# A decoder layer on one core: x loaded transposed with its rows between the chunks, and the retention's key and value projections beside the lower half of the sparse attention

## The chip, the cores and the metric

The kernel runs on one core of a Trainium2 chip. Its engines are TensorE (PE; weight loads PEld), VectorE (DVE), ScalarE (ACT), GpSimd (POOL) and SyncE (SP, which here only issues DMA transfers); each takes its own instructions in order and waits on semaphores for the others. The metric is device time in microseconds (us) of one execution.

## The reference, cut to what matters

One layer on x of 1024 rows by 1024 columns in fp32: an RMS norm, one wide input projection, three groups of heads, a SiLU gate, an output projection, a residual add and a last norm.

```python
u = rms_norm(h, attn_norm[layer])
proj = jnp.einsum('bsd,dc->bsc', u, w_in[layer])
(dq, dk, dv, sq, ckv, iq, ik, iw, rq, rk, rv, gate) = jnp.split(proj, split_points, axis=-1)
...
o_a = diff_attention(dq, dk, dv, ...)          # 6 heads, two softmaxes each
o_b = dsa_attention(sq, rms_norm(ckv), iq, ik, iw, w_uk, w_uv, top_k)   # 8 index heads pick 256 keys per query
o_c = retention(rotary(rq), rotary(rk), rv, ret_norm[layer])            # 4 heads, chunks of 128
y = jax.nn.silu(gate) * mixed
h = h + jnp.einsum('bsc,cd->bsd', y, w_out[layer])
```

RMS norm divides each row of x by the root of its mean square and multiplies each column by a gain.

## The kernel before

u is kept transposed (columns of x on the partitions, rows along the free axis) as two fp32r tiles, `uh` (the rounded value) and `ul` (the rest), each [128, 8 chunks, 1024 rows]. Weights are split in the same way, and every projection multiplies three times: high by high, high by low, low by high. `split` does it: a copy to the high part, a subtraction for the low.

**Front.** `setup` loads x in eight blocks of 128 rows (tiles `x`, on SP's queue) and, after the first two, the weights of the differential attention's values and of the index keys and head weights (`wide`, 456 columns). `prep_a` squares and sums a block on ACT, works out 1/rms in `rstd_small` (tiny operations on ACT and DVE), and multiplies the block by 1/rms and by the gain (`gb`, broadcast to all partitions) on DVE. `prep_b` transposes it on PE in eight 128x128 pieces (L220) and splits the result from PSUM into `uh` (ACT) and `ul` (DVE). Then `gemm` runs the 456 columns, row block by row block: 8 x 8 x 3 = 192 matmuls of 128x456 (L282 to L284). `dv_evac` takes each block from PSUM: the values `v`, the index keys `kt`, which are transposed into `kkh` and `kkl`, and the head weights `iw`.

**Index stage.** `iq0` to `iq3` are projections of the index queries; `idx_scores` makes the scores from them and `kkh`, `kkl`.

**Middle stage.** Three streams are interleaved: the differential attention (`diff`, L651), the top-k search with its ties, and the remaining projections in the order of K's strings `order` and `order2` (g: gates, q and k: differential queries and keys, s: sparse queries, ck: the latent, M: what is made of it, r: the retention's query, key and value). `rv` and `rk` are the last two of them: 192 matmuls of 128x256 each (L282 to L284 again).

**Lower half of the sparse attention.** `dsa(p, 0)` for three pairs of heads takes the four lower row blocks: 24 steps, each of score matmuls (L720, L721), a softmax on DVE (L728, L736) and ACT (L729), transposes on PE (L611) and value matmuls (L626). Beside it run the ties of the other blocks and a third stream: `retention(0)`, then `out_weights`, which loads w_out in sixteen pieces through two buffers (`wr`) and splits them into `woh` and `wol`, and part of the output projection of block 7 (`project`, L935 to L937). `woh` and `wol` take the memory of `uh` and `ul`, so their first write waits for the last matmul that reads u.

**Upper half.** `dsa(p, 1)`, 24 steps on the four larger blocks, beside `retention(1)` and two projected blocks; then the rest of the projection.

What sets the order: the code emits the streams by `interleave`, which takes next from the stream that has used the smallest share of its planned cost (`wd`, `wt`, `wg`, `gw` ... in K), and a scheduler at build time places the instructions on each engine by a model of their readiness; inside `manual_schedule` the named engines keep the order of the code.

Of the kernel before, what the change touches and what calls it, by code (L numbers as in the profile page):

```python
# [10 lines left out]
F = mybir.dt.float32  # L11
# [7 lines left out]
S = 1024  # L19
# [12 lines left out]
K = {'mk': 'up ky', 'mp': 's2 g5 g4', 'rt': ('hl', 'pq'), 's0': ('gg', 'gg', 'ag', 'gg', 'vg', 'gg', 'vg', 'vg'), 'xp': 2, 'bufs': (8, 3, 3, 5, 3, 4, 1), 'pp': (7,), 'rot': 0, 'order': 'g0 g1 k1 q1 k2', 'order2': 'q2 g2 rq g6 s0 ck g7 s1 M g3 rv rk | ', 'wd': 36, 'wt': 13, 'wg': 119, 'gw': 56, 'rw': 26, 'rx': 132, 'pw': 40, 'ow': 84, 'nf': 2, 'ev': 200, 'late': 8, 'de': ('aa', 'aa', 'aa'), 'da': 'ax', 'gd': (7, 4, 2), 'hlp': 'sqkk', 'tkp': '', 'vt': 'v', 'rs': 'x', 'nv': 1, 'dn': 'v', 'ws': 'gg', 'oe': ('av', 'gg'), 'one': 0, 'idx': (42, 40), 'iqs': 'iq2 iq3 q0 k0'}  # L32
# [36 lines left out]
class Trunk:  # L69
# [65 lines left out]
    def setup(self):  # L135
# [4 lines left out]
        self.gb = self.ptile(1024)  # L140
        nc.scalar.dma_start(self.gb, bass.AP(tensor=i["attn_norm"].tensor, offset=i["attn_norm"].offset,
                                             ap=[[0, 128], [1, 1024]]))
        self.x = {}
        for b in range(NB):
            self.x[b] = self.slot("x", [128, 1024])
            nc.sync.dma_start(self.x[b], i["x"][0, b * 128:(b + 1) * 128, :])
            if b == K["xp"] - 1:
                self.wide()
# [13 lines left out]
    def setup_late(self):  # L162
# [25 lines left out]
        m1 = self.sb.tile([128, NB, 72], F, name="trigdec", tag="m1")  # L188
# [4 lines left out]
    def rstd_small(self, ss, n, tag):  # L193
# [7 lines left out]
        nc.vector.scalar_tensor_tensor(q, r, v, r, op0=OP.mult, op1=OP.mult)  # L201
# [4 lines left out]
    def prep_a(self, b):  # L206
        nc = self.nc
        xt = self.x[b]
        junk = self.half("junk", [128, 1024], BF)
        ss = self.sb.tile([128, 1], F, name=self.name("ss"), tag="ss", bufs=2)  # L210
        nc.scalar.activation(junk, xt, AF.Square, accum_out=ss)
        r = self.rstd_small(ss, D, "rs1")
        nc.vector.scalar_tensor_tensor(xt, xt, r, self.gb, op0=OP.mult, op1=OP.mult)

    def prep_b(self, b):
        nc = self.nc
        xt = self.x.pop(b)
        p = self.pS()
        for k in range(KC):
            nc.tensor.transpose(p[:, k * 128:(k + 1) * 128], xt[:, k * 128:(k + 1) * 128], self.ident)  # L220
# [759 lines left out]
```

## Time and profile before

| | |
|---|---|
| runs | 785.86, 781.14, 777.98 us; median 781.14 us |
| profiled execution | 785.29 us, of which the span on the page is 783.6 us |
| PE, PEld | 724.2 us (92%), 597.4 us (76%) |
| DVE, ACT, POOL | 551.5 us (70%), 447.6 us (57%), 311.5 us (40%) |
| moved by DMA | 113.05 MB, 144 GB/s over the span |
| matmuls of the 512-wide projections (L130 to L132) | 3 x 352, 141.6, 139.4 and 140.7 us busy |

The page shows busy time by engine; matmuls are pipelined, so two that overlap are both counted to their ends, and a full PE can still be slow. A view by stages shows in which stretch an engine had room, at what granted clock PE ran and what the transfers moved. A row of the timeline gives the start, the length, the line, the operation with its tiles (out<-in), and in brackets how long the engine had stood and who released it. In the views by line, the numbers are a count, then busy time and mean, or the least, median and greatest length in ns.

### The profile page before, as it was taken

How to read it: one execution, taken by the hardware profiler on the slowest of the kernel's cores; microseconds unless marked ns; L12 is line 12 of the kernel's file. 1: busy time of each engine (PE TensorE's matmuls, PEld its weight loads, DVE VectorE, ACT ScalarE, POOL GpSimd, SP SyncE). 2: the span in 40 equal slices, each digit the busy share in tenths (PEclk: the TensorE clock that was granted, in tenths of full speed). 3: DMA queues.
4: the chain of work that ended last, by engine and by line, in shares of the span. 5: the costliest groups of instructions: out<-in, count | busy, mean ns of one | idle time of the engine just before them, and what ended most of it. 6: DMA issues, size and time to landing. Idle time of an engine off the chain costs nothing.

```text
span 783.6 us, 12891 instructions
## 1 busy us (share of the span) xinstructions
PE 724.2 (92%) x4314; PEld 597.4 (76%) x4314; DVE 551.5 (70%) x1312; ACT 447.6 (57%) x989; POOL 311.5 (40%) x343
## 2 busy tenths in 40 slices
PE   3999999999999999988799789998978999999996
PEld 3798888887887898766577567997855887787884
DVE  5920277789999989999889997325657766664443
ACT  4531255559888968787755566434356656554332
POOL 6401322225434438557347699335733242120000
PEclk9999999999999999999899999999968999999999
DMA  9303645454374352461274476564578974413351
GB/s 332 78 1 71 197 136 145 139 137 132 99 218 115 85 163 78 120 169 35 67 206 144 144 215 190 158 192 160 158 213 236 281 200 127 123 48 108 118 176 59
DMA packets 93250, 113.05 MB, mean 144 GB/s; under 512 B 11904, under 2 KB 63488, under 8 KB 93056
## 3 DMA queue, kind: packets, MB, share of 16 engines
q1 hardware_dynamic: 91888, 109.61, 48.1%
q10 hardware_dynamic: 1296, 2.62, 0.9%
q8 instruction: 34, 0.56, 0.3%
q14 instruction: 32, 0.26, 0.1%
HBM read 75.50 MB, written 36.18 MB: 143 GB/s over the span
## 4 chain that ended last, share of the span: by engine, by line
PE 61%; DVE 16%; DMA 6%; issue 6%; POOL 5%; ACT 4%; SPq 0%; DVEq 0%; POOLq 0%; ACTq 0%
PE pB L626 6%; PE pG L130 6%; PE pG L132 6%; PE pG L131 5%; PE pB L611 4%; PE pG L282 4%; PE pG L936 4%; PE pG L937 4%; PE pG L935 4%; PE pG L283 4%; PE pG L284 4%; DVE jv L378 3%; DMA wr<-in_w_in_dram 2%; PE pS L344 2%; PE pS L343 2%
## 5 line engine op out<-in xcount | busy, mean ns | idle before, releaser
L130 PE MATMUL pG<-uh,wh 128*128 128x512 f32 x352 | 141.6, 402 | 1.8 <-DVE gt L827 1.8
L132 PE MATMUL pG<-uh,wl 128*128 128x512 f32 x352 | 140.7, 400 | 0.6 <-POOL wl L123 0.6
L131 PE MATMUL pG<-ul,wh 128*128 128x512 f32 x352 | 139.4, 396 | 0.0
L123 POOL TENSOR_TENSOR wl<-wr,wh 128x512 fp32r<-128x512 f32 x56 | 79.3, 1430 | 106.3 <-PE pG L131 69.4
L392 ACT ACTIVATE ja<-sc,tk_c 128x896 int8<-128x896 f32 (+2 forms) x93 | 83.2, 895 | 17.3 <-DVE tk_c L399 12.0
L113 ACT ACTIVATE pt<-pB 128x512 f32<-128x512 f32 (+2 forms) x120 | 58.8, 496 | 43.8 <-PE pB L611 43.5
L130 PEld LDWEIGHTS pG<-uh,wh 128*128 128x128 f32 x352 | 66.8, 190 | 16.4 <-DVE gt L827 2.4
L132 PEld LDWEIGHTS pG<-uh,wl 128*128 128x128 f32 x352 | 66.4, 189 | 16.1 <-POOL wl L123 0.9
L611 PE MATMUL pB<-ident,pp 128*128 128x128 f32 x432 | 72.9, 287 | 5.5 <-DVE gt L758 3.4
L626 PE MATMUL pB<-pt,v 128*64 128x128 f32 x864 | 70.8, 302 | 7.6 <-ACT pt L113 7.0
L131 PEld LDWEIGHTS pG<-ul,wh 128*128 128x128 f32 x352 | 66.7, 189 | 13.0 <-issue 0.2
L626 PEld LDWEIGHTS pB<-pt,v 128*64 128x64 f32 x864 | 57.7, 147 | 18.9 <-ACT pt L113 9.5
L378 DVE TENSOR_SCALAR_CACHE_REDUCE jv<-sc,tk_c 128x640 bf16<-128x640 f32 (+4 forms) x81 | 69.2, 855 | 1.0
L611 PEld LDWEIGHTS pB<-ident,pp 128*128 128x128 f32 x432 | 51.2, 144 | 22.2 <-issue 9.1
L677 POOL TENSOR_SCALAR pq<-pq,mx 128x896 f32<-128x896 f32 (+7 forms) x48 | 43.2, 901 | 58.6 <-DVE mx L676 55.8
L119 POOL TENSOR_SCALAR wh<-wr 128x512 fp32r<-128x512 f32 x56 | 37.8, 680 | 59.9 <-DMA wr<-in_w_in_dram 54.3
L282 PE MATMUL pG<-wh,uh 128*128 128x256 f32 x192 | 55.0, 288 | 2.6 <-POOL wh L119 2.6
L283 PE MATMUL pG<-wl,uh 128*128 128x256 f32 x192 | 54.9, 286 | 0.0
L284 PE MATMUL pG<-wh,ul 128*128 128x256 f32 x192 | 54.3, 284 | 0.0
L346 ACT ACTIVATE pp<-pS 128x1024 f32<-128x1024 f32 (+5 forms) x48 | 36.5, 760 | 31.1 <-PE pS L344 31.0
L651 PE MATMUL pS<-st,st 128*128 128x512 f32 (+3 forms) x144 | 43.3, 368 | 11.5 <-DVE mx L662 8.9
L351 DVE SCALAR_TENSOR_TENSOR sc<-pp,iw,sc 128x1024 f32<-128x1024 f32 (+5 forms) x42 | 43.5, 1044 | 14.3 <-ACT pp L346 13.6
(218 smaller groups left out, 1756.1 us busy)
## 6 DMA issues: line engine op xcount, KB each, us to landing
wr<-in_w_in_dram SPq DMA_DIRECT2D x56, 256.0 KB, 3.2
st<-qdq SPq DMA_DIRECT2D x24, 256.0 KB, 4.2
st<-qkk SPq DMA_DIRECT2D x18, 256.0 KB, 5.9
x<-in_x_dram SPq DMA_DIRECT2D x8, 512.0 KB, 6.6
qiq<-hl SPq DMA_DIRECT2D x16, 256.0 KB, 3.5
st<-qiq SPq DMA_DIRECT2D x8, 512.0 KB, 3.3
wr<-in_w_out_dram SPq DMA_DIRECT2D x16, 256.0 KB, 3.4
xr<-in_x_dram SPq DMA_DIRECT2D x8, 512.0 KB, 3.5
```

The source lines that it names most:

```text
L113: self.nc.scalar.activation(out, in_, AF.Copy)
L123: (self.nc.vector if e2 == "v" else self.nc.gpsimd).tensor_tensor(lo, src, hi.bitcast(F), OP.subtract)
L130: mm(ps, wh, xh, start=start, stop=False)
L131: mm(ps, wh, xl, start=False, stop=False)
L132: mm(ps, wl, xh, start=False, stop=stop)
L282: mm(ps, uh, hs[k], start=k == 0, stop=False)
L283: mm(ps, uh, ls[k], start=False, stop=False)
L284: mm(ps, ul, hs[k], start=False, stop=k == KC - 1)
L378: nc.vector.tensor_scalar(jv[:, :nv[b]], hb if b == 7 and bit >= 16 else sc[b], t, 0.0, op0=op, op1=OP.add, accum_out=cnt[:, j:j + 1])
L392: nc.scalar.activation(ja[:, :nv[b]], sc[b], AF.Sign, bias=cut(b), scale=-1.0, accum_out=cnt[:, cols[b]:cols[b] + 1])
L611: nc.tensor.transpose(p[:, k], pr[:, (k0 + k) * 128:(k0 + k + 1) * 128], self.ident)
L626: self.last = nc.tensor.matmul(o[u * 64:(u + 1) * 64], vals[k], pts[g, a][:, k, u * 128:(u + 1) * 128], start=k == (i if u else 0), stop=k ...
```

## The change

The host now also passes x transposed (`x_t`), the 456 weight columns as one array (`w_dv`) and the gain as a column per chunk (`gk`). `setup` loads the eight chunks of `x_t` (tiles `x`, the first two in halves) on SP's queue with the eight blocks of rows of x between them, and the weights on ACT's queue; `square` sums the squares of each row block on ACT. `front` multiplies before the norm is known: `split_x` makes `uh` and `ul` from x times gain, and for each chunk as it comes PE runs 18 matmuls for six row blocks, which take six PSUM banks. Row blocks 6 and 7 follow in a second pass over the chunks. 1/rms of the rows (`rn`) multiplies these results as they leave PSUM (`evac`). For all other projections u must hold the norm: `row_rms` spreads 1/rms over the partitions with eight matmuls of ones by diagonal tiles (`diags`), and `resplit` multiplies x by gain and 1/rms and splits it again, first rows 0 to 511, then 512 to 1023. The order on PE, DVE and SP in `front` is that of the code. `keys` (the transposes of the index keys) stands between iq0 and iq1.

In K, `order2` was `'q2 g2 rq g6 s0 ck g7 s1 M g3 rv rk | '` and is `'q2 g2 rq g6 s0 ck g7 s1 M g3 | rv rk'`: what stands behind the bar is run ahead of `retention(0)` in the third stream of the lower half. That stream's planned cost `gw` goes from 56 to 97. `s0`, which names the engines that split each chunk of the 456 columns, uses POOL and ACT and no longer DVE.

```diff
+        self.gk = self.const("gk", [128, KC])
+        nc.scalar.dma_start(self.gk, i["attn_norm"])
+        self.wide()
+        self.x, self.rows = [], []
+        self.ss = self.const("ss", [128, NB])
+        for k in range(KC + 1):
+            if k < KC:
+                t = self.slot("x", [128, S])
+                for c in (slice(0, 512), slice(512, S)) if k < 2 else (slice(0, S),):
+                    nc.sync.dma_start(t[:, c], i["x_t"][k * 128:(k + 1) * 128, c])
+                self.x.append(t)
+            for b in ((k - 1,) if 0 < k else ()):
+                row = self.ptile(D) if b % 2 else self.wtile("row", [D], F)
+                nc.sync.dma_start(row, i["x"][0, b * 128:(b + 1) * 128, :])
+                self.rows.append(row)
+                self.square(b)
...
+    def split_x(self, k):
+        g = self.gk[:, k:k + 1]
+        for c in (slice(0, 512), slice(512, S)):
+            hi, x = self.uh[:, k, c], self.x[k][:, c]
+            nc.scalar.activation(hi, x, AF.Copy, scale=g)
+            nc.vector.scalar_tensor_tensor(self.ul[:, k, c], x, g, hi.bitcast(F), op0=OP.mult, op1=OP.subtract)
...
+    def row_rms(self):
+        p = self.pS()
+        for b in range(NB):
+            nc.tensor.matmul(p[:, b * 128:(b + 1) * 128], self.ct, self.dg[b], start=True, stop=True)
...
+            self.nc.vector.tensor_scalar(self.dg[b], self.ident, self.rn[:, b:b + 1], None, op0=OP.mult)
...
+    def resplit(self, p, half):
+        c = slice(half * 512, half * 512 + 512)
+        for k in range(KC + 1):
+            if k < KC:
+                x = self.x[k][:, c]
+                nc.vector.scalar_tensor_tensor(x, x, self.gk[:, k:k + 1], p[:, c], op0=OP.mult, op1=OP.mult)
+                nc.scalar.activation(self.uh[:, k, c], x, AF.Copy)
+            if k:
+                hi = self.uh[:, k - 1, c]
+                nc.vector.tensor_tensor(self.ul[:, k - 1, c], self.x[k - 1][:, c], hi.bitcast(F), OP.subtract)
...
+        for k in range(KC):
+            self.split_w(k)
+            self.split_x(k)
+            if k == KC - 1:
+                self.diags()
+            step(range(6), k)
+        for b in range(6):
+            evac(b, ps[b])
+        rb = self.row_rms()
+        self.resplit(rb, 0)
+        ps[6:] = [self.pG()[:, :WA] for _ in range(2)]
+        for k in range(KC):
+            step((6, 7), k)
+        for b in (6, 7):
+            evac(b, ps[b])
+        self.resplit(rb, 1)
+        return keys
...
+            r = self.rn[:, b:b + 1]
+            nc.scalar.activation(self.v[:, b, :], ps[:, 0:384], AF.Copy, scale=r)
+            nc.scalar.activation(kt[:, b], ps[:, 384:456], AF.Copy, scale=r)
...
-        for b in range(NB):
-            self.prep_a(b)
-            self.prep_b(b)
-        drain(self.gemm(("a", C_DV, WA, self.dv_evac())))
-        with self.tc.manual_schedule(engines={mybir.EngineType.PE}):
-            drain(units("iq0 iq1"))
+        with self.tc.manual_schedule(engines={et.PE, et.DVE, et.SP}):
+            keys = self.front()
+        with self.tc.manual_schedule(engines={et.PE}):
+            drain(units("iq0"))
+            keys()
+            drain(units("iq1"))
```

How the instructions move, at three places (`order` rows: line, operation, out<-in, shape, count). The first is PE from the start of the program: `pS` receives the transposes of row blocks `x`, `pG` the 456 columns of one row block. Before:

```order
L220 MATMUL pS_129<-ident,x_77 128x128 x8
L220 MATMUL pS_151<-ident,x_79 128x128 x8
L282 MATMUL pG_321<-wb_299,uh 128x456
L283 MATMUL pG_321<-wb_301,uh 128x456
L284 MATMUL pG_321<-wb_299,ul 128x456
```

And PE in the changed kernel where the last chunk ends: `pB_164` is row block 5, `pS_387` the spread 1/rms, `pG_420` and `pG_421` are row blocks 6 and 7.

```order
L272 MATMUL pB_164<-wb_153,uh 128x456
L272 MATMUL pB_164<-wb_157,uh 128x456
L272 MATMUL pB_164<-wb_153,ul 128x456
L233 MATMUL pS_387<-dg_347,ct 128x128 x4
L233 MATMUL pS_387<-dg_352,ct 128x128 x4
L272 MATMUL pG_420<-wb_152,uh 128x456
L272 MATMUL pG_421<-wb_152,uh 128x456
```

The transposes at the head are gone; the spread of 1/rms stands between the first six row blocks and the last two.

The second place is PE at the end of rk in the kernel before (`pG_5371` is rk's last row block, `pS` are score steps of the lower half):

```order
L282 MATMUL pG_5371<-wh_5128,uh 128x256
L283 MATMUL pG_5371<-wl_5129,uh 128x256
L284 MATMUL pG_5371<-wh_5128,ul 128x256
L626 MATMUL pB_5839<-pt_5812,v_5629 64x128 x3
L611 MATMUL pB_5863<-ident,pp_5821 128x128
L720 MATMUL pS_5903<-st_5890,st_5891 128x512
L721 MATMUL pS_5903<-st_5890,st_5891 128x512
L720 MATMUL pS_5922<-st_5890,st_5891 128x128
L721 MATMUL pS_5922<-st_5890,st_5891 128x128
```

And PE inside rk's last row block (`pG_6137`) in the changed kernel, whose L347 to L349, L787, L788, L693 and L678 are the same operations:

```order
L347 MATMUL pG_6137<-wh_5893,uh 128x256
L348 MATMUL pG_6137<-wl_5894,uh 128x256
L787 MATMUL pS_5657<-st_5651,st_5652 128x384
L693 MATMUL pB_5526<-pt_5493,v_5066 64x128 x3
L678 MATMUL pB_5562<-ident,pp_5500 128x128 x3
L788 MATMUL pS_5657<-st_5651,st_5652 128x384
L349 MATMUL pG_6137<-wh_5893,ul 128x256
L347 MATMUL pG_6137<-wh_5903,uh 128x256
```

Nine of the lower half's 24 score steps stood ahead of rk's last matmul; now 17 do, spread through rv and rk.

The third place is ACT at the first copy into `woh`. Before (`pp` and `mx` are a step's softmax, `pt` its transposed result):

```order
L113 ACTIVATE pt_5812<-pB_5827 128x4x128
L729 ACTIVATE pp_5900,mx_5899<-pp_5900,mx_5899 128x384
L113 ACTIVATE woh<-wr_5722 128x512
L113 ACTIVATE pt_5862<-pB_5863 128x128
L113 ACTIVATE pt_5862<-pB_5868 128x2x128
```

In the changed kernel (L796 is the same softmax):

```order
L113 ACTIVATE pt_5561<-pB_5562 128x3x128
L796 ACTIVATE pp_5588,mx_5587<-pp_5588,mx_5587 128x256
L113 ACTIVATE woh<-wr_6183 128x512
L113 ACTIVATE pt_5561<-pB_5579 128x4x128
L796 ACTIVATE pp_5661,mx_5660<-pp_5661,mx_5660 128x384
```

The copy stood ahead of the softmax of the lower half's tenth step, and stands ahead of that of the seventeenth now.

## Rows read from the trace of the kernel before

**Rows 1.** Stages of the whole span: length, each engine's busy us, PEclk, DMA share, GB/s.

```profile
0.00:10.00 10.00, 0.08 (x1) 0.11 (x2) 2.67 (x16) 4.00 (x8) 2.44 (x9) 1.00 0.79 274
10.00:20.00 10.00, 7.76 (x30) 6.87 (x31) 8.54 (x10) 4.92 (x9) 10.00 (x11) 1.00 1.05 392
...
30.00:40.00 10.00, 8.77 (x41) 7.63 (x42) 9.19 (x26) 4.05 (x12) 0.75 (x1) 0.83 0.01 3
...
176.00:494.00 318.00, 293.79 (x1694) 238.51 (x1693) 291.69 (x739) 235.97 (x535) 182.43 (x190) 0.97 0.49 136
...
494.00:525.00 31.00, 31.00 (x268) 29.46 (x267) 8.76 (x32) 13.71 (x39) 9.10 (x10) 1.00 0.55 175
...
546.00:559.50 13.50, 13.50 (x113) 12.75 (x113) 6.72 (x14) 1.38 (x4) 11.49 (x18) 1.00 0.37 116
559.50:602.50 43.00, 34.72 (x211) 24.30 (x210) 27.63 (x91) 23.83 (x64) 14.27 (x16) 0.80 0.75 215
```

**Rows 2.** PE's timeline in the front: start us, us, line, operation, count.

```profile
9.92 1.94 PE L220 MATMUL pS<-ident,x 128*128 128x128 f32 x8 [9.92 <-DVE rs L198]
...
28.24 1.04 PE L220 MATMUL pS<-ident,x 128*128 128x128 f32 x8
...
33.50 0.58 PE L282 MATMUL pG<-wb,uh 128*128 128x456 f32 x1
33.88 0.58 PE L283 MATMUL pG<-wb,uh 128*128 128x456 f32 x1
...
63.88 0.37 PE L282 MATMUL pG<-wb,uh 128*128 128x456 f32 x1
64.08 0.37 PE L283 MATMUL pG<-wb,uh 128*128 128x456 f32 x1
...
67.10 0.39 PE L130 MATMUL pG<-uh,wh 128*128 128x512 f32 x1
...
78.36 0.40 PE L130 MATMUL pG<-uh,wh 128*128 128x512 f32 x1
```

**Rows 3.** The chain of waits around rk's weights: start us, us, what.

```profile
525.67 5.51 DMA wr<-in_w_in_dram
```

**Rows 4.** Groups by line, first 70 us: count, busy us, mean ns, idle before.

```profile
L213 DVE SCALAR_TENSOR_TENSOR x<-x,rs,pp 128x1024 f32<-128x1024 f32 x8 | 13.0, 1628 | 0.2
...
L123 DVE TENSOR_TENSOR ul<-pS,uh 128x1024 fp32r<-128x1024 f32 x8 | 9.7, 1217 | 5.1 <-ACT uh L113 5.1
```

**Rows 5.** Timeline of ACT and DVE, the first row block: start us, us.

```profile
6.01 1.06 ACT L211 ACTIVATE junk<-x 128x1024 bf16<-128x1024 f32 x1 [3.93 <-DMA x<-in_x_dram]
...
8.49 1.28 DVE L213 SCALAR_TENSOR_TENSOR x<-x,rs,pp 128x1024 f32<-128x1024 f32 x1
```

**Rows 6.** Two lines and tile woh: count, ns min/median/max, first and last start.

```profile
L441 PE MATMUL pB<-f,bd x12: 590/592/697, 295.9 to 537.0; 128*128 128x512 f32 x12
...
L448 DVE SCALAR_TENSOR_TENSOR f<-f,c_diff_norm,f x6: 751/1414/1632, 303.0 to 546.0; 128x512 f32<-128x512 f32 x6
...
L123 DVE TENSOR_TENSOR wol<-wr,woh x8: 672/689/1540, 560.5 to 610.0; 128x512 fp32r<-128x512 f32 x8
...
L113 ACT ACTIVATE woh<-wr x8: 616/629/631, 559.4 to 609.3; 128x512 fp32r<-128x512 f32 x8
...
L119 POOL TENSOR_SCALAR woh<-wr x8: 617/648/805, 559.5 to 610.4; 128x512 fp32r<-128x512 f32 x8
...
L123 POOL TENSOR_TENSOR wol<-wr,woh x8: 1267/1279/1609, 560.2 to 611.2; 128x512 fp32r<-128x512 f32 x8
```

**Rows 7.** PE's timeline in rv, and thirty value matmuls near the end.

```profile
494.77 0.29 PE L282 MATMUL pG<-wh,uh 128*128 128x256 f32 x1
494.89 0.28 PE L283 MATMUL pG<-wl,uh 128*128 128x256 f32 x1
...
717.02 1.96 PE L626 MATMUL pB<-pt,v 128*64 128x128 f32 x30
```

**Rows 8.** ACT's timeline behind rk: start us, us, idle before, and releaser.

```profile
559.43 0.63 ACT L113 ACTIVATE woh<-wr 128x512 fp32r<-128x512 f32 x1 [9.90 <-PE pG L283]
```

More of the change, by code (lines that the diff above doesn't have):

```diff
@@ L216, in prep_b, with square @@
+    def square(self, b):
+        junk = self.half("junk", [128, D], BF)
+        self.nc.scalar.activation(junk, self.rows[b], AF.Square, accum_out=self.ss[:, b:b + 1])
+    def row_rms(self):
         nc = self.nc
-        xt = self.x.pop(b)
         p = self.pS()
-        for k in range(KC):
-            nc.tensor.transpose(p[:, k * 128:(k + 1) * 128], xt[:, k * 128:(k + 1) * 128], self.ident)
-        pv = p.rearrange("p (k s) -> p k s", k=KC)
-        sl = slice(b * 128, (b + 1) * 128)
-        self.split(self.uh[:, :, sl], self.ul[:, :, sl], pv)
+        for b in range(NB):
+            nc.tensor.matmul(p[:, b * 128:(b + 1) * 128], self.ct, self.dg[b], start=True, stop=True)
+        return p
@@ new lines, in diags @@
+    def diags(self):
+        self.rn = self.rstd_small(self.ss, D, "rs8")
+        self.dg = []
+        for b in range(NB):
+            if b % 4 == 0:
+                dgs = self.half("dg", [128, 4, 128])
+            self.dg.append(dgs[:, b % 4])
+            self.nc.vector.tensor_scalar(self.dg[b], self.ident, self.rn[:, b:b + 1], None, op0=OP.mult)
+    def resplit(self, p, half):
+        nc = self.nc
+        c = slice(half * 512, half * 512 + 512)
[7 more added lines that the diff above has]
+                nc.vector.tensor_tensor(self.ul[:, k - 1, c], self.x[k - 1][:, c], hi.bitcast(F), OP.subtract)
@@ new lines, in front, with step @@
+    def front(self):
+        nc = self.nc
+        hs, ls = self.wsplit(C_DV, WA)
+        evac, keys = self.dv_evac()
+        mm = nc.tensor.matmul
+        big = [self.pS(), self.pS()]
+        ps = [big[b // 2][:, b % 2 * 512:b % 2 * 512 + WA] for b in range(4)] + [self.pB()[:, :WA] for _ in range(2)]
+        ps += [None, None]
+        def step(blocks, k):
+            st, sp = k == 0, k == KC - 1
+            todo = [[(b, self.uh, hs, st, False) for b in blocks], [(b, self.uh, ls, False, False) for b in blocks],
+                    [(b, self.ul, hs, False, sp) for b in blocks]]
+            order = [t for b in zip(*todo) for t in b] if sp else [t for w in todo for t in w]
+            for b, u, w, s0, s1 in order:
+                mm(ps[b], u[:, k, b * 128:(b + 1) * 128], w[k], start=s0, stop=s1)
+        for k in range(KC):
+            self.split_w(k)
[14 more added lines that the diff above has]
+        return keys
@@ L231, in wide @@
     def wide(self):
-        raws = []
+        self.dvw = []
         for k0 in range(0, KC, 2):
@@ L249, in wsplit @@
             ls = [big[2 + k // 2][:, k % 2] for k in range(KC)]
-            for k in range(KC):
-                self.split(hs[k], ls[k], self.dvw[k // 2][:, k % 2], *K["s0"][k])
+            self.split_w = lambda k: self.split(hs[k], ls[k], self.dvw[k // 2][:, k % 2], *K["s0"][k])
             return hs, ls
```

63 lines of the change are left out of this document (26 added, 37 removed).

## The prediction

> **What bounds the kernel now.** I read the stages first [rows 1]. TensorE is busy for 724 of 783.6 us, so idle engines elsewhere matter little; what can be won is the time in which PE is idle, slow, or not yet started. The stages differ. The index scores up to 176 us stay the same work in the same order. From 176 to 494 us DVE has 292 of 318 us busy: that stage is set by DVE and the chains around it, and in the order its instructions stand as before, so I only shift it. Two places are left, and the change is at both. The first is the front, up to 67 us. PE starts at 9.92 us, does its first transposes with gaps, and falls to the lower clock after it has stood: at 33 us the 128x456 matmuls follow each other every 0.38 us, where the granted clock of 30 to 40 us averages 0.83 (a mix of 1.2 and 2.4 GHz), against 0.206 us later [rows 1, 2]. The second is 494 to 602.5 us: rv and rk run there with PE full, except for a wait of some 7 us for rk's weights (a load of 5.51 us, then a split) [rows 3], and what follows, 559.5 to 602.5 us, has PE at 34.7 of 43 us with a granted clock of 0.80 and only 211 matmuls, where 113 fit in the 13.5 us before [rows 1].
>
> **The front, before.** 192 matmuls of 128x456 at 0.206 us are 39.6 us; 64 transposes, eight in 1.04 us or, without the tail of the last, 0.87, are 7 us [rows 2]. From the first transpose to iq0's first matmul at 67.10 us there are 57.2 us, so some 11 us are gaps and slow clock. iq1 starts at 78.36 us [rows 2], and that is the point I compare.
>
> **The front, after.** The 64 transposes go, with their eight copies on ACT, eight subtractions (1.22 us) and eight normalizations (1.63 us) on DVE [rows 4]. x arrives twice: 4.19 MB transposed and 4.19 MB in rows; with 1.87 MB of value weights and 0.52 MB for iq0 that is 10.8 MB ahead of or with the last row block. The traffic of before, 274 GB/s in the first 10 us and 392 in the next [rows 1], gives 6.66 MB by 20 us and the rest by 30.6 us; the last transposed chunk, 9.2 MB in, lands at about 26.5 us. The first half-chunk is half of the 512 KB transfer that ACT had at 6.01 us [rows 5]; with a split behind it PE starts at about 6 us.
>
> PE: six blocks x eight chunks x three = 144 matmuls, 29.7 us, plus 1.6 us for some nine at 0.38 us at the start, before the clock rises: 37.2 us. A chunk feeds 18 matmuls, 3.7 us, and arrives about every 2.8 us (the 1.05 MB of a chunk and its row block at 392 GB/s), so PE, not the transfer, sets this once it runs. Per chunk ACT needs two copies of 0.63 us [rows 6] and a square of 1.06 us [rows 5], DVE two operations of about 0.65 us: both hidden below 3.7 us. The row statistics (30.6; the square and small operations, 2.5 us from 6.01 to 8.49 in the trace [rows 5]; then eight diagonal products of about 0.25 us) are ready at about 35 us, 2 us early; that is their cover. Ahead of them DVE waits for the tiny load of c_diff_norm, behind it for dl, both queued among these loads on SP; dl should land at about 36 us.
>
> Eight fp32 matmuls with ones broadcast 1/rms: the 128x512 one lasts 0.59 us [rows 6], so 0.9 us (a quarter each) to 4.7 us (full price); I take 2: 39.2 us. Now u is multiplied again, in two halves: 32 DVE operations of 128x512. Nearest rows: 0.61 us (half of 1.22 [rows 4]), 0.67 to 0.69 and 0.75 us [rows 6]; I take 0.65, so 10.4 us a half. PE covers the first half with blocks 6 and 7 (48 matmuls, 9.9 us, to 49.1). ACT has their four evictions ahead of the half's last copy, so that half is complete at 51.8. iq0's first half (5.5 us) runs in the cover of the second, which ends at 51.8 + 10.4 + 1.3 = 63.5 us; three matmuls and eight key transposes later, 65.2 us, iq1 starts. Against 78.36 that is **13 us**. Bounds: 14.5 us with 0.61 us per DVE operation; 6 us if the loads run at 274 GB/s throughout (10.8 MB by 39.4, statistics 7 us late).
>
> One row speaks against the 0.65: the fused multiply of 128x512 has a minimum of 0.75 but a median of 1.41 and a maximum of 1.63 us [rows 6], the long ones beside a busy POOL, and POOL splits iq1's weights (four operations, 0.65 and 1.28 us each [rows 6]) during the second half. The Trainium skill, SBUF — State Buffer, section "SBUF: two separate sides", says that DVE and GpSimd share one port pair under an exclusive lock, taken also by DVE operations with two SBUF inputs, so that one side waits out the other's instruction. By that rule the four POOL operations would be added in full and the front would give 9 us; the row's long operations agree with it.
>
> From the rows alone: the multiply here reads one operand from PSUM and the 0.67 us operation of [rows 6] had POOL beside it too (the same view: both split the output weights), so I keep 13 us; POOL's 3.9 us added to the second half is a rival below.
>
> **rv and rk, moved.** The 384 matmuls of 0.12 us (46 us) [rows 7] are the same; what changes is what stands between them, as the order rows of the section on the change show: 17 instead of 9 of the 24 score steps of the lower half stand ahead of rk's last matmul. Eight steps on PE are 16 score matmuls (2.3 us by columns), 16 transposes (1.7) and 16 value matmuls (1.0 at 1.96 us for thirty [rows 7]): 5 us more up to rk's end, which makes 65 + 5 = 70 us if the chains hide behind the 2.4 us of rv/rk matmuls per step. Behind rk's end stood 15 steps in 43 us; now seven. Why 43 us? ACT's copy into woh overwrites u and therefore waits for rk's last matmul: 9.90 us in which the steps queued behind it on ACT stood too [rows 8]; then 16 loads of the output weights pass two buffers, until the last split at 611 us [rows 6]. These loads still cannot start before rk's end, so I leave that stretch its 43 us. What it gains is content: from rk's end to the first output-projection matmul PE has 154 matmuls before and 216 after, 16 and 28 us at the spacings above. **12 us gained there, 5 given in rv/rk, net 7 us.** SP's queue keeps the same number of transfers; rv's weights stay where they were in it, rk's second pair moves behind a few stores of rd, so the 7 us wait stays. Bounds: +18 us if each of the eight steps is worth 43/15 = 2.9 us behind rk; 0 if the pace of the loads stays and 28 more projection matmuls (6.6 us) fall behind the last step, as the order has them.
>
> **Sum.** 783.6 - 13 - 7 = 763.6 us span; the profiled execution took 785.29 us, so 765.3. The median of the runs shown is 781.14, 0.5% lower: 765.3 x 781.14 / 785.29 = **761 us**.
>
> **Rivals.**
> *POOL in the way.* 3.9 us more in the second half: front 9, total 16: 765 us. For it: the 1.41 and 1.63 us [rows 6]. Against: the 0.67 us operations.
> *Front only.* The retention part nets 0: 781 - 13 = 768 us. For it: the weight loads set the stretch behind rk, and nothing speeds them up. Against: PE there is mostly waiting, so content moved out of it should shorten the part not bound by loads.
> *The loads set the front.* At 274 GB/s the statistics are 7 us late: front 6, total 13: 768 us. For it: 10.8 MB where 7.1 were loaded (x, value weights, the norm's gain, iq0). Against: 392 GB/s in 10 to 20 us [rows 1].
> *Both at their better bound.* 14.5 + 18: 749 us. For it: the 0.80 clock and 211 matmuls in 43 us leave much room [rows 1]. Against: the load chain.
> *Slower.* PE takes its instructions in order; if the scores-to-transposes chain is not hidden behind rv/rk, each of the 17 steps adds up to 2.9 us: 49 + 46 + 10 of waits (65 us less the 55 of matmuls in rv/rk now) = 105 instead of 65 us. That is 40 lost against 25 gained: 796 us. It decides from 1.5 us exposed per step. Against it: 494 to 525 us, where rv and the last diff steps share PE at 31.00 of 31 us [rows 1].
>
> **How the numbers follow.** Chances: forecast (752 to 764) 0.45, POOL in the way 0.10, front only 0.17, loads set the front 0.12, both at the better bound 0.10, slower 0.03, and 0.03 for a loss of another kind. Eight in ten: 747 to 775 us; the forecast's own range is 752 to 764. About 1% (8 us) is what can be told from no change here: faster means below 773.3. Forecast, POOL and the better bound count whole for faster (0.65), most of the two 768 cases too (0.21 of 0.29, as 768 lies 5 us from the line): 0.86; same 0.10; slower 0.04.
>
> **What would show it.** Right: the first 128x456 matmul near 6 us; row statistics before the sixth block ends; iq1 starting near 65 us; the stage from the first diff score to rv shifted by 13 us with its length kept; score steps spread evenly through rv/rk, which then last about 70 us; first projection matmul still about 43 us behind rk's end, with more matmuls in between. Wrong: slow (0.38 us) spacing beyond the first microseconds, PE waiting for the diagonals or for uh's halves longer than 2 us, DVE operations of 1.4 us in the second half, rv/rk above 80 us, or w_out loads ending later than 52 us after rk.

## The result, and the profile after

The changed kernel takes 773.34 us (median of 4 runs, 771.78 to 775.24) where the kernel before took 783.5 us beside it (4 runs): ratio 0.987, 95% interval 0.9836 to 0.9904, so 1.3% faster. The forecast was 761 us, or 2.6% below the median it started from, with 752 to 764 us as its own range: the sign was right, the size was about twice what came, and the time lies outside the range. Times of kernels are medians of executions in the usual, fast state; a few slow ones (one of 2979.96 us) are left out. The profiled execution took 775.24 us, its span is 773.5 us (783.6 before).

First the page's busy times, then the stages, with the columns of [rows 1].

```profile
PE 718.1 (93%) x4266; PEld 592.1 (77%) x4266; DVE 558.1 (72%) x1315; ACT 457.9 (59%) x1002; POOL 311.7 (40%) x343
```

```profile
0.00:10.00 10.00, 3.27 (x9) 2.90 (x10) 3.90 (x14) 4.81 (x7) 3.83 (x11) 1.00 0.79 274
10.00:20.00 10.00, 10.00 (x45) 8.98 (x44) 4.03 (x4) 6.32 (x12) 10.00 (x10) 1.00 1.03 408
30.00:40.00 10.00, 10.00 (x54) 9.13 (x53) 3.81 (x16) 5.55 (x15) 5.16 (x6) 1.00 0.39 115
164.00:484.40 320.40, 295.63 (x1693) 239.73 (x1693) 291.13 (x737) 235.06 (x534) 180.62 (x189) 0.96 0.50 135
484.40:515.00 30.60, 30.59 (x261) 28.79 (x260) 14.68 (x55) 17.80 (x52) 8.71 (x11) 1.00 0.63 198
556.30:606.90 50.60, 41.65 (x299) 31.98 (x296) 34.66 (x91) 30.17 (x70) 19.10 (x20) 0.87 0.79 231
606.90:674.00 67.10, 66.36 (x509) 53.52 (x510) 42.13 (x94) 36.93 (x80) 18.43 (x25) 1.00 0.48 142
674.00:765.50 91.50, 89.60 (x476) 71.54 (x475) 43.52 (x97) 34.27 (x82) 9.63 (x13) 1.00 0.38 121
```

Against [rows 1], PE now works from 6.73 us on and is full from 10 to 40 us at clock 1.00, where it had 8.77 us at 0.83 between 30 and 40. The middle stage (first differential score to rv) is 320.4 us long, 317.7 before. The stretch from rk's last matmul to the first output-projection matmul was the 43 us of the last of [rows 1]. It is now 556.3 to 606.9, so 50.6 us, and its granted clock is still below 1.

Where the 10.1 us of span come from, by the starts in the two timelines: iq1 starts 12.6 us earlier (65.72, against 78.36 [rows 2]), the first differential score 12.6 us earlier (164.0, 176.7), rv 9.9 us earlier (484.4, 494.3), the end 10.1 us earlier. **The front's gain reaches the end less what the middle stage gave back, and between rv's start and the end nothing is gained at all.** That last part is best read as four stretches. Beside each length stands the time that its matmuls take when they follow each other without gaps, counted over the trace's records with spacings of full stretches (0.12 us for 128x256, 0.23 for 512 columns, 0.11 a transpose, 0.066 a record of a value matmul, 0.1 to 0.21 a record of the retention's), and the difference, which I call idle. It holds gaps, waits and slow clock alike.

| us: length (work; idle) | before | after |
|---|---|---|
| rv's first matmul to rk's last | 65.2 (59.1; 6.0) | 71.9 (65.4; 6.5) |
| rk's last to the first projection matmul | 43.0 (21.3; 21.8) | 50.6 (30.2; 20.3) |
| first projection matmul to the last score | 93.9 (88.7; 5.2) | 67.1 (63.4; 3.7) |
| last score to the last projection matmul | 79.7 (78.0; 1.7) | 92.0 (88.2; 3.9) |
| sum | 281.9 (idle 34.7) | 281.5 (idle 34.4) |

Work has moved from the third row to the others. The idle time stayed where it was, some 20 us of it behind rk, and its sum is what it was. In that second row PE is not busy at all for 8.3 us before (43.00 less 34.72) and 9.0 us now (50.60 less 41.65); the rest is slow clock and loose spacing.

The count needs care. A value product of the kernel stands as two records in the trace, 864 for the 432 that the code issues, and so do the retention's products:

```profile
L626 PE MATMUL pB<-pt,v 128*64 128x128 f32 x864 | 70.8, 302 | 7.6 <-ACT pt L113 7.0 <-DVE pt L115 0.6
```

The expectations below count such a product once, at about the price of one record. So their work is too small and their idle time too large: the 24.2 us of work behind rk in the changed kernel is 30.2, and their 26 us of idle time there is some 20.

Now the views that show why the second row grew. The output weights' tile, as in [rows 6]: count, ns min/median/max, first and last start.

```profile
L113 ACT ACTIVATE woh<-wr x8: 614/629/634, 556.2 to 603.7; 128x512 fp32r<-128x512 f32 x8
L119 POOL TENSOR_SCALAR woh<-wr x8: 617/620/1139, 556.3 to 603.1; 128x512 fp32r<-128x512 f32 x8
L123 POOL TENSOR_TENSOR wol<-wr,woh x8: 1265/1276/1657, 557.0 to 603.9; 128x512 fp32r<-128x512 f32 x8
L123 DVE TENSOR_TENSOR wol<-wr,woh x8: 677/692/1711, 557.6 to 605.6; 128x512 fp32r<-128x512 f32 x8
```

The waits in that stretch: who waited, for whom, us in total, times, longest.

```profile
POOL woh L119 <- DMA wr<-in_w_out_dram: 27.6, 7, 5.2
...
ACT woh L113 <- DMA wr<-in_w_out_dram: 5.0, 5, 2.8
...
DVE wol L123 <- ACT woh L113: 3.6, 3, 2.6
...
PE pB L678 <- DVE gt L825: 3.2, 2, 2.7
...
PE pG L587 <- DMA rt<-rd: 1.6, 1, 1.6
...
ACT woh L113 <- PE pG L348: 0.5, 1, 0.5
```

SP's timeline in it (start, us, what it issued, how many), with the loads of the output weights among the steps' transfers.

```profile
578.38 2.13 SPq L969 DMA_DIRECT2D wr<-in_w_out_dram  x2
580.59 0.39 SPq L383 DMA_DIRECT2D st<-qsq  x1
581.03 0.42 SPq L383 DMA_DIRECT2D st<-qkk  x1
...
584.15 9.47 SPq L969 DMA_DIRECT2D wr<-in_w_out_dram  x4
594.81 0.33 SPq L383 DMA_DIRECT2D st<-qsq  x1
...
598.39 0.42 SPq L980 DMA_DIRECT2D fn<-in_final_norm_dram  x1
598.87 0.43 SPq L988 DMA_DIRECT2D yr<-yd  x1
```

And the chain of waits through it: start, us, what.

```profile
585.59 5.10 DMA wr<-in_w_out_dram
590.77 1.15 POOL woh L119
591.99 1.28 POOL wol L123
593.29 2.65 DMA wr<-in_w_out_dram
...
598.87 4.99 DMA yr<-yd
...
606.87 0.49 PE pG L1003
```

The reader is to see two things. The splits span 556.2 to 606 us, 50 us, where it was 53 (559.4 to 612), and what paces them is load, split, next load: POOL waits 27.6 us for the loads (18.8 before), SP stands 9.47 us over four of them with a step's transfer behind. And the 9.90 us in which ACT stood with its copy into woh until rk was done [rows 8] is gone (0.5 us): the stall that the forecast named did disappear, and bought nothing.

### The profile page after: what moved, and what is told of

Same layout as the page of the kernel before. It is cut to its first block, busy times and chain, and to the rows that moved or that the text cites. A ratio compares the mean times of both kernels' runs of the same rounds, so it can differ in the third digit from the quotient of the medians.

```text
span 773.5 us, 12824 instructions
## 1 busy us (share of the span) xinstructions
PE 718.1 (93%) x4266; PEld 592.1 (77%) x4266; DVE 558.1 (72%) x1315; ACT 457.9 (59%) x1002; POOL 311.7 (40%) x343
## 4 chain that ended last, share of the span: by engine, by line
PE 51%; DVE 17%; DMA 11%; ACT 7%; issue 7%; POOL 3%; SPq 2%; ACTq 0%; DVEq 0%; POOLq 0%
PE pB L693 4%; PE pG L1003 4%; PE pG L1004 4%; PE pG L130 4%; PE pG L1005 4%; PE pG L132 4%; PE pG L131 4%; DVE jv L443 4%; PE pB L678 3%; PE pS L272 3%; ACT ja L457 3%; PE pS L409 2%; DVE pp L747 2%; PE pS L408 2%; DMA wr<-in_w_out_dram 2%
## 5 line engine op out<-in xcount | busy, mean ns | idle before, releaser
L113 ACT ACTIVATE pt<-pB 128x512 f32<-128x512 f32 (+2 forms) x120 | 58.8, 495 | 42.2 <-PE pB L678 42.0
L132 PEld LDWEIGHTS pG<-uh,wl 128*128 128x128 f32 x352 | 67.1, 191 | 16.9 <-POOL wl L123 2.8
L678 PE MATMUL pB<-ident,pp 128*128 128x128 f32 x432 | 72.3, 286 | 6.1 <-DVE gt L825 3.2
L693 PE MATMUL pB<-pt,v 128*64 128x128 f32 x864 | 68.7, 297 | 9.6 <-ACT pt L113 7.9
L693 PEld LDWEIGHTS pB<-pt,v 128*64 128x64 f32 x864 | 56.2, 145 | 21.0 <-ACT pt L113 10.1
L119 POOL TENSOR_SCALAR wh<-wr 128x512 fp32r<-128x512 f32 x56 | 40.3, 723 | 73.0 <-DMA wr<-in_w_in_dram 60.3
L678 PEld LDWEIGHTS pB<-ident,pp 128*128 128x128 f32 x432 | 51.4, 144 | 20.8 <-issue 7.6
L744 POOL TENSOR_SCALAR pq<-pq,mx 128x896 f32<-128x896 f32 (+7 forms) x48 | 38.7, 807 | 56.8 <-DVE mx L743 42.9
L411 ACT ACTIVATE pp<-pS 128x1024 f32<-128x1024 f32 (+5 forms) x48 | 36.5, 760 | 31.7 <-PE pS L409 31.6
L347 PE MATMUL pG<-wh,uh 128*128 128x256 f32 x192 | 55.1, 289 | 0.0
L349 PE MATMUL pG<-wh,ul 128*128 128x256 f32 x192 | 54.6, 285 | 0.0
```

The lines of the kernel that those rows point to most:

```text
L113: self.nc.scalar.activation(out, in_, AF.Copy)
L132: mm(ps, wl, xh, start=False, stop=stop)
L347: mm(ps, uh, hs[k], start=k == 0, stop=False)
L349: mm(ps, ul, hs[k], start=False, stop=k == KC - 1)
L678: nc.tensor.transpose(p[:, k], pr[:, (k0 + k) * 128:(k0 + k + 1) * 128], self.ident)
L693: self.last = nc.tensor.matmul(o[u * 64:(u + 1) * 64], vals[k], pts[g, a][:, k, u * 128:(u + 1) * 128], start=k == (i if u else 0), stop=k ...
```

## The experiments

"Front alone" is the changed kernel with rv and rk in their old place. The question was which part of the change gives the 1.3%, and where the move's 7 us went.

**One part at a time.**

```diff
 (front alone: the changed kernel with)
-'order2': '... M g3 | rv rk', 'gw': 97
+'order2': '... M g3 rv rk | ', 'gw': 56
 (move alone: the kernel before with)
-'order2': '... M g3 rv rk | ', 'gw': 56
+'order2': '... M g3 | rv rk', 'gw': 97
```

> The new front, with the retention's value and key projections back in their old place (ahead of the lower half, share 56 as before). The forecast's step (the move is worth 7 us): about 7 us slower than the changed kernel, some 780 us, ratio to the kernel before 0.996, and the first output-projection matmul some 43 us behind rk's end. The rival 'front only' (the move nets 0): the same as the changed kernel within 2 us, ratio 0.985 to 0.989, with the same 10 to 13 us gained up to the first differential score.

> The old front, with only the retention's value and key projections moved beside the lower half (share 97). The forecast's step: 7 us faster than the kernel before, ratio 0.991. The rival 'front only': ratio 0.998 to 1.002; the first output-projection matmul then stands 50 us or more behind rk's end instead of 43, and what is done earlier (the scores) comes back as a longer run of projections after the last score.

Front alone: 772.61 us, ratio 0.9863 (0.9816 to 0.991). Move alone: 790.28 us, ratio 1.0078 (1.0043 to 1.0113). So the front carries the whole gain, and the move by itself is not worth 7 us but costs some 6 on the old front. The stretch behind rk (columns as above; front alone, then move alone, in two fences):

```profile
548.20:590.40 42.20, 33.30 (x211) 22.99 (x211) 29.08 (x92) 23.72 (x64) 14.28 (x16) 0.84 0.79 221
```

```profile
566.50:621.60 55.10, 39.99 (x298) 30.74 (x296) 35.92 (x91) 30.43 (x69) 18.78 (x20) 0.91 0.73 214
```

With rv and rk in the old place the stretch is 42.2 us, and ACT stands 10.7 us in it before woh, as in [rows 8]:

```profile
ACT woh L113 <- PE pG L348: 10.7, 1, 10.7
```

With the move it holds 298 matmuls in 55.1 us. Its length follows what stands in it.

**Front alone and changed kernel side by side**, five rounds on one chip, the same two kernels again.

> The changed kernel once more, beside the front alone on the same chip, so that the two can be told apart by less than 1%. Theory 'the move displaces, it does not fill' (idle time of TensorE behind rk is a sum of its own, to which moved work is added): the two agree within 3 us. The forecast's step: this one is 7 us faster than the front alone.

> The front alone once more, for the same comparison: within 3 us of the changed kernel if the move only displaces work; 7 us slower if the forecast's step holds; some 6 us faster if the move costs on the new front what it cost on the old one (ratio 1.0078).

Changed kernel 774.53 us (0.9895, 0.9851 to 0.9939), front alone 769.4 us (0.9827, 0.9789 to 0.9865). The move costs here too: 5 us, where I had put 0 to 3; the first sets of the two kernels, not taken beside each other, had shown 0.7 us (773.34 and 772.61). The four stretches of these two profiled executions are within 0.5 us of their first ones, save for 1 us behind rk in the front alone, and sum to 281.2 and 279.7 us, so only 1.5 of the 5 us show there. The profiled executions themselves are only 2.4 us apart (773.71 and 771.27), and 1.9 of that is already there at the first differential score (165.6 and 163.7 us); the rest I can't place. The middle stage is no place for it: its length runs from 317.1 to 321.7 us over all sixteen profiles, in no order of kernels (before 317.7, move alone 321.7; changed kernel 320.4 and 317.5; front alone 320.2 and 318.6). The 2.7 us that it "lost" above lie within that.

**Half of the move**: rv ahead of the lower half, rk beside it.

```diff
-'order2': '... M g3 | rv rk', 'gw': 97
+'order2': '... M g3 rv | rk', 'gw': 76
```

> Half of the move: the value projection stays ahead of the lower half, the key projection stands beside it (share 76). 15 score tiles then stand ahead of rk's end (9 in the front alone, 17 in the changed kernel) and 25.4 us of TensorE work between it and the first projection matmul. If moved work only displaces (idle time of 26 us there, whatever the work): the stretch lasts 51 us and the time is that of the changed kernel within 3 us, 770 to 775. The forecast's step (the stretch keeps its 43 us): 766 to 769 us.

775.06 us (0.9894, 0.9845 to 0.9942). The stretch is 55.9 us with 31.6 us of work, so 24.3 idle: more than the 20 us of idle time on top of the work, and nothing of the 43 us.

**The output weights without the load chain.** These two kernels leave out the splits and use `woh` for `wol` too.

```diff
-                raw = self.rtile([512])
-                nc.sync.dma_start(raw, i["w_out"][0, k * 128:(k + 1) * 128, c])
-                self.split(self.woh[:, k, c], self.wol[:, k, c], raw, *e)
...
+            self.mv(self.woh[:, k], self.qd["sq0"][k % 2].rearrange("c p s -> (c p) s"))
```

> The changed kernel, but the output weights come as 8 plain transfers of 512 KB straight into woh (from a tile that was split earlier; as many bytes), without the two small buffers and the splits, and wol is woh: so the output product is left out as a true one, its matmuls are all there. Theory 1 (the chain load, split, next load sets when the projection can start, and so how the stretch behind rk is filled): first projection matmul within 25 us of rk's end instead of 51 (4.19 MB at 240 GB/s are 17 us), and the time falls by 10 to 20 us, to 753 to 763. Rival (PE's total work behind rk is the bound, or the scores' own chains leave the gaps): the projection starts earlier, but the time falls by less than 4 us.

> The front alone (retention's projections in their old place) with the same plain transfers into woh, the product left out as a true one as there. If the move was worth nothing only because the load chain of the output weights held the projection (theory 1), it pays once that chain is gone: this kernel is 4 to 8 us slower than the same with the move. If the move is worth nothing in itself, the two agree within 2 us.

With the move 769.73 us (0.9823, 0.9765 to 0.9881), without it 763.86 us (0.976, 0.9712 to 0.9807). The stretch behind rk, changed kernel and front alone, in two fences:

```profile
558.10:578.90 20.80, 16.73 (x127) 11.62 (x125) 10.71 (x42) 10.81 (x31) 1.88 (x4) 0.92 0.98 338
```

```profile
545.40:579.70 34.30, 28.72 (x218) 20.47 (x218) 23.92 (x89) 21.34 (x60) 1.88 (x4) 1.00 0.97 304
```

Theory 1 was half right. The load chain does decide when the projection starts: 20.8 us behind rk's end instead of 50.6. But the time falls by 4 us, not 10 to 20: idle time behind rk falls from 20.3 to 9.0 us, but 3 us more stand idle in rv and rk, and 3 us more between the first projection matmul and the last score, where most of the work now stands (109.4 us where there were 67.1). And the move still does not pay; it costs 5.9 us. In the front alone PE's granted clock stays at 1.00 through the stretch (0.84 with the chain), and idle falls from 20.9 to 12.2 us: that is the part that the chain and the splits cost. DMA is busy for 0.97 of it, so loads that begin at rk's end could not have gone much faster.

**The same with all of the computation: wide loads, prefetch, another queue.** Eight loads of 512 KB into three buffers that the differential stage has left (`pq`); then the first three of these rows loaded while rv and rk run; and, apart from these, the sixteen small loads issued by POOL.

```diff
-                raw = self.rtile([512])
-                nc.sync.dma_start(raw, i["w_out"][0, k * 128:(k + 1) * 128, c])
+            raw = self.sb.tile([128, D], F, name=self.name("wr"), tag="pq", bufs=NPQ)
+            nc.sync.dma_start(raw, i["w_out"][0, k * 128:(k + 1) * 128, :])
...
 (prefetch: W loads rows 0 to 2; front alone: '... M g3 rv rk | W')
-'order2': '... M g3 | rv rk'
+'order2': '... M g3 | rv W rk'
 (POOL's queue, small loads)
-                nc.sync.dma_start(raw, i["w_out"][0, ...
+                nc.gpsimd.dma_start(raw, i["w_out"][0, ...
```

> The changed kernel, with the output weights loaded as 8 rows of 512 KB into three buffers that the differential stage has left, and split in halves by the same engines: all of the computation is there. Theory 1, in the size that the plain transfers showed (the two-buffer load chain costs 4 to 9 us behind rk): 764 to 770 us, POOL waits for these loads under 10 us instead of 27.6, first projection matmul 33 to 43 us behind rk's end. Rival (only the splits' own work counted in the plain runs, not the wait for the loads): 771 to 775.

> The front alone with the same wide loads of the output weights; all of the computation is there. Theory 1: 763 to 768 us, first projection matmul 30 to 37 us behind rk's end instead of 42.5; if the move costs once the load chain is out of the way, as the plain transfers had it (5.9 us), this is some 5 us faster than the same with the move, and the fastest of all with the whole computation. If the move only displaces, the two agree within 2 us.

> The changed kernel with the wide loads, and the first three of the eight rows of the output weights loaded between the retention's value and key projections, so that they lie ready when rk's last matmul frees u; all of the computation is there. In the program order 14.5 us of TensorE work then stand between rk's end and the first projection matmul (24.2 in the changed kernel). Theory 1 (the loads hold the stretch): first projection matmul 28 to 35 us behind rk's end, 765 to 769 us. Rival (what is idle there belongs to the scores' own chains and is only moved): the projection starts as early, but 769 to 773 us, since the idle time turns up in the stretches behind.

> The changed kernel with its 16 loads of the output weights issued by POOL instead of SP, everything else as it is; in the program order only 5 us of TensorE work then stand between rk's end and the first projection matmul. If SP's queue, in which the loads stand between the steps' own transfers, sets their pace: first projection matmul within 25 us of rk's end and 766 to 771 us. If the two small buffers and the splits set it: TensorE waits for woh at the projection for 10 us or more, and 773 to 778 us.

> The front alone with the loads of the output weights issued by POOL; the program order keeps 17.2 us of TensorE work ahead of the first projection matmul. If SP's queue sets the pace of the loads: 2 to 5 us faster than the front alone, 766 to 769 us, the projection 33 to 38 us behind rk's end. If not: 770 to 773 us and 41 to 43 us.

> The front alone, with wide loads of the output weights, of which the first three rows are loaded while rv and rk run (as in the changed kernel with prefetch): all of the computation is there. If the move is worth nothing in itself: within 3 us of the changed kernel with prefetch (769), first projection matmul about 33 us behind rk's end (16.2 us of TensorE work and 17 us idle). If the move pays 7 us once the loads lie ready: 776. If it costs, as the plain transfers had it: 763 to 765.

> The changed kernel with the prefetch once more, beside the front alone with the prefetch, on the same chip: 766 to 771 us, first projection matmul 31 us behind rk's end. Its distance to the front alone with prefetch is what the move is worth when its supposed partner, the wait for the output weights, is largely gone: 0 within 3 us if the move only displaces work, 7 us faster if the forecast's step holds there, 4 us or more slower if the move costs.

| | with the move | front alone |
|---|---|---|
| as it is (one chip) | 774.53 (0.9851 to 0.9939) | 769.4 (0.9789 to 0.9865) |
| plain transfers, no splits | 769.73 (0.9765 to 0.9881) | 763.86 (0.9712 to 0.9807) |
| wide loads | 770.56 (0.9786 to 0.9876) | 770.87 (0.9799 to 0.9888) |
| loads on POOL's queue | 769.84 (0.9774 to 0.9868) | 769.48 (0.9765 to 0.9862) |
| prefetch | 769.03 and 771.48 (0.9798 to 0.9881) | 772.11 (0.9821 to 0.9889) |

The two kernels of each row ran on one chip, except the first of the prefetch (the interval is the second's). Nowhere is the move 7 us faster: it lies between 0.6 us faster and 6 us slower, the old front with it. Most of what I expected of these runs came in the stretch and not in the time. By the theory that the loads hold the stretch, wide loads were to take 764 to 770 us with the move and 763 to 768 without, the prefetch 765 to 769 with the move; they took 770.56, 770.87, and 769.03 and 771.48. With wide loads the projection started 42.2 us behind rk with the move (33 to 43 expected), but POOL still waited 19.2 us for its loads where I had put under 10; in the front alone they gave nothing (39.2 us, 30 to 37 expected). POOL's queue in the front alone missed too: 40.5 us and no gain, where 33 to 38 and 2 to 5 us were expected. The prefetch there started the projection 37.1 us behind rk, 33 expected. What the prefetch and POOL's queue did to the stretch is the sharpest result. The stretch behind rk with prefetch, with POOL's queue, and the stretch that follows there up to the last score:

```profile
554.60:586.00 31.40, 24.88 (x166) 18.47 (x164) 25.22 (x65) 20.81 (x51) 19.10 (x20) 0.89 0.79 236
```

```profile
554.40:567.10 12.70, 10.82 (x68) 8.01 (x66) 7.82 (x27) 6.42 (x18) 5.97 (x10) 0.73 0.81 227
567.10:681.30 114.20, 108.44 (x817) 86.29 (x818) 81.86 (x183) 67.70 (x151) 44.96 (x59) 0.97 0.63 181
```

With prefetch POOL's wait for the loads is 9.4 us, where it was 27.6:

```profile
POOL woh L119 <- DMA wr<-in_w_out_dram: 9.4, 4, 3.0
```

The projection begins 31.4 and 12.7 us behind rk's end instead of 50.6. Much less work then stands ahead of it, too: 17.8 and 7.0 us, where it was 30.2. The idle time of the four stretches, in order, is 8.5, 13.5, 5.6 and 2.0 us with prefetch and 7.7, 5.8, 15.0 and 3.1 us with POOL's queue: 29.8 and 31.6 in sum, 34.4 in the changed kernel. With POOL's queue 14.5 us of idle time leave the stretch behind rk, and 11.3 turn up between the first projection matmul and the last score. With prefetch 6.8 us leave it, and 2 each turn up in rv and rk and behind the first projection matmul; the repeat (35.5 us behind rk's end, 31 expected) loses 2.7 there, gains 3.7 in rv and rk, and has 35.6 in sum. Over the sixteen profiles the sum lies between 26.2 and 37.0 us, and only the two kernels without splits and the first prefetch are below 30.

No version with all of the computation is better than the front alone by more than the intervals allow. **Front alone, 769.4 us on the chip where the changed kernel took 774.53, is the version that I would keep**; prefetch, wide loads and POOL's queue reach the same 769 to 773.

## Why the prediction was half right

**The front: right, step by step.** PE's timeline of the changed kernel (start, us, line, operation, count):

```profile
6.73 1.86 PE L272 MATMUL pS<-wb,uh 128*128 128x456 f32 x4 [6.73 <-ACT uh L222]
...
11.43 1.40 PE L272 MATMUL pS<-wb,ul 128*128 128x456 f32 x4
...
39.00 0.37 PE L272 MATMUL pB<-wb,ul 128*128 128x456 f32 x1
39.21 1.95 PE L233 MATMUL pS<-dg,ct 128*128 128x128 f32 x16
40.92 1.07 PE L272 MATMUL pG<-wb,uh 128*128 128x456 f32 x4
...
61.06 0.50 PE L131 MATMUL pG<-ul,wh 128*128 128x512 f32 x1 [0.30 <-DVE ul L255]
...
64.93 1.04 PE L646 MATMUL pB<-ident,kt 128*64 128x128 f32 x8
65.72 0.47 PE L130 MATMUL pG<-uh,wh 128*128 128x512 f32 x1
```

- PE starts at 6.73 us (6 forecast); the pass over six row blocks ends at 39.2 (37.2 forecast). It had no gap; the slow spacing of 0.38 us lasted until 12.2 us, for fourteen matmuls instead of nine (0.9 us), and the late start (0.7 us) is most of the rest.
- The row statistics were ready in time: the spread of 1/rms follows the pass without a gap. It ends at 40.92, 1.7 us later (2 forecast).
- The first half of u was complete at 53.2 us (51.8 forecast): the multiplication began 2 us later (41.2), and the half's last copy on ACT stood behind the evictions of blocks 6 and 7, as forecast (rows below). The second half, done at 64.3 us (63.5 forecast), is paced by DVE, as forecast: PE waits 0.3 to 0.4 us on it four times.
- iq1 starts at 65.72 us (65.2 forecast), **a gain of 12.6 us where 13 were forecast**. The front alone confirms it end to end: 10.7 to 13.6 us by its two ratios (0.9863 and 0.9827 of some 783.6 us).

The loads did not set the front (408 GB/s from 10 to 20 us, PE full), so that rival is out. POOL in the way is out at its price, though its mechanism is there. DVE's timeline as the first half ends, then POOL's, then the end of the half on ACT and DVE:

```profile
48.36 0.74 DVE L251 SCALAR_TENSOR_TENSOR x<-x,gk,pS 128x512 f32<-128x512 f32 x1
49.02 1.16 DVE L255 TENSOR_TENSOR ul<-x,uh 128x512 fp32r<-128x512 f32 x1
50.10 0.73 DVE L251 SCALAR_TENSOR_TENSOR x<-x,gk,pS 128x512 f32<-128x512 f32 x1
50.76 1.11 DVE L255 TENSOR_TENSOR ul<-x,uh 128x512 fp32r<-128x512 f32 x1
...
48.33 2.99 POOL L123 TENSOR_TENSOR wl<-wr,wh 128x512 fp32r<-128x512 f32 x2 [10.17 <-PE pG L272]
...
50.51 0.58 ACT L636 ACTIVATE v<-pG,rs 128x384 f32<-128x384 f32 x1 [0.73 <-PE pG L272]
...
51.86 0.65 ACT L252 ACTIVATE uh<-x 128x512 fp32r<-128x512 f32 x1
...
52.53 0.69 DVE L255 TENSOR_TENSOR ul<-x,uh 128x512 fp32r<-128x512 f32 x1 [0.33 <-ACT uh L252]
```

While POOL's two subtractions run, the subtraction that reads both operands from SBUF takes 1.16 and 1.11 us instead of its median of 0.68; the multiply that reads one operand from PSUM keeps its 0.73. POOL's two other operations there held up no DVE operation by more than 0.1 us, and its last two came after the half. So it cost DVE 0.9 us, not 3.9, and even that was covered: the half's last subtraction waited for ACT's copy, which stood behind the evictions. The Trainium skill, SBUF — State Buffer, section "SBUF: two separate sides", has the lock taken by DVE operations with two SBUF inputs; these rows agree with that on which operation is held up. The price was 0.48 and 0.43 us, a part of POOL's instruction each time and not the whole of it, which is where the 3.9 us of the rival went wrong; and it fell in the first half, not in the second.

**rv and rk: right.** 71.9 us from rv's first to rk's last matmul (70 forecast), with 17 instead of 9 score tiles ahead of rk's end. The forecast's 5 us of added work was too small: the thirty value matmuls of [rows 7] are records, so sixteen products are 32 records and 2.1 us, not 1.0; by the table the work grows by 6.3 us. And in the "wait of some 7 us for rk's weights" PE itself stood for 2.6 us; other matmuls filled the rest, so there was less to fill than I had read. Before, in PE's timeline:

```profile
532.00 0.51 PE L282 MATMUL pG<-wh,uh 128*128 128x256 f32 x2 [2.56 <-POOL wh L119]
```

The rival "slower" is out: the chain of the steps hides behind rv and rk.

**The stretch behind rk: the step that failed.** "I leave that stretch its 43 us. What it gains is content" was wrong twice. The content was mis-sized: by the trace's records it grows from 21.3 to 30.2 us, 8.9 and not 12. And the stretch did not keep its 43 us: it grew by 7.6, to 50.6, so its idle time stayed at some 20 us and the content came on top. I had reasoned that waiting PE can take in work without getting longer. It could have if the added work ran in the waits. It did not, as five kernels with the small buffers and SP's queue show: 41.2 to 43.0 us with 21.3 of work, 50.2 to 55.9 with 30.1 to 31.6, and 20 to 25 us idle in all of them. Part of that idle time is the chain of loads and splits: without it the front alone has 12.2 us there, not 20.9. The rest of the cause is argued: each score step has a chain of its own from scores to softmax to transposes, the in-order queues (PE's, and SP's with the loads of the output weights among the steps' transfers) put loads, splits and steps in one row, and the upper half's steps, more of which now stand in this stretch, bring transfers of 256 and 512 KB into it (11.7 MB in all against 9.3 MB before).

**The tail.** The forecast had 28 more projection matmuls (6.6 us) behind the last score only as a bound, and kept a net gain. By the trace 19 more stand there and, which it had not counted, 48 more records of the retention: the work grew by 10.2 us, the time by 12.3 (79.7 to 92.0), so 2.1 us more idle. In sum +6.7, +7.6, -26.8 and +12.3 us: nothing left of the 7 us.

**Rivals and base.** The rival "front only", 768 us at 0.17, was the case. What I held against it, that PE mostly waits there and so can take in work, is the argument that fell. Even this rival was somewhat too good, since the move costs up to 6 us. Two more microseconds lie in the base: the 781.14 us that I started from is the median of three runs, and that of all later sets lies between 783 and 784.3. The wrong signs that I had named were a poor net: the loads of the output weights did not end later than 52 us after rk (50), rv and rk did not pass 80 us, and no DVE operation of 1.4 us stood in the front. Only the 43 us showed it.

**Open.** Why the move costs 5 to 6 us in three pairs and nothing in three others, when the stretches account for 1 to 4 us of it; whether another share `gw` would place the moved work better, since it was changed together with the order each time; and what the 26 to 37 us of idle time behind rv's start would need, since starting the projection up to 38 us earlier does not remove them.

## What to carry to other kernels

A stretch in which PE is partly idle does not by itself take in more work for free: here some 20 us of idle time stayed, and the work was added to it. Before work is moved to fill a hole, ask whose chain made the hole and whether that chain is still in it afterwards. Count a stretch as work plus its own idle time, sum that over all the stretches up to the end, and price the move by the sum, not by the stretch that looks emptiest. Check first whether a price per row of the trace is one per product of the code: here two rows stood for one product. An early start that takes full work forward, as in the front here, keeps its value to the end.

## What the runs showed of the hardware that was not expected

- From 6.73 to 12.2 us the 128x456 matmuls followed each other every 0.38 us, from 12.5 us on every 0.21, although the row for 0 to 10 us gives a granted clock of 1.00. The trace's first record of the clock begins at 12.32 us, so that row has none under it; there the spacing tells the level. In the stretch behind rk the row does show it: 0.84 in the front alone with the load chain, where PE stood for up to 2.4 us, 1.00 with plain transfers, where it never stood for longer than 1.2 us.
- A DVE subtraction of 128x512 with both inputs in SBUF took 1.11 to 1.16 us beside a POOL subtraction (0.68 otherwise), POOL's own 1.30 and 1.73 us (median 1.29 before); a DVE multiply with one input in PSUM beside the same POOL operation took 0.73 to 0.74 us.
- A middle stage with the same work runs between 317.1 and 321.7 us from one profiled execution to the next: a difference of 3 us in one pair of traces there says nothing.
